# The end of a layer in a two-layer decoder trunk: norm rows by a broadcasting DMA, statistics by column halves, the last quarter later, and the next layer's first stages tile by tile

## The chip, the core and the metric

The program runs on one core of one Trainium2 chip, in one launch. The metric is device time in microseconds (us), the median of three runs. A profile of one execution was taken by the hardware profiler; a granted TensorE clock of 1.00 in it means the upper of that engine's two levels, 2.4 GHz, and 0.50 the lower one, 1.2 GHz.

## The reference, cut to what matters

```python
def mixer(x, w_in, ...):                      # three attentions of h = x @ w_in, gated and merged
    h = x @ w_in                              # x [256, 1024], w_in [1024, 5316]
    ...
    return merged @ w_o

def moe(x, ...):                              # 16 experts, best group of 4, top 2 in it
    ...
    for e in range(N_EXPERTS):
        he = jax.nn.silu(xt @ w_gate[e]) * (xt @ w_up[e])
        y = y + combine[:, e:e + 1] * (he @ w_down[e])
    return y

def layer_norm(x, g, b):
    mu = mean(x, -1);  var = mean((x - mu) ** 2, -1)
    return (x - mu) * rsqrt(var + 1e-5) * g + b

for l in range(2):
    x = layer_norm(ALPHA * x + mixer(x, ...), ln1_g[l], ln1_b[l])
    x = layer_norm(ALPHA * x + moe(x, ...), ln2_g[l], ln2_b[l])      # the change sits here
```

All is float32, 256 tokens by 1024 columns.

## The kernel before, in words

The 256 tokens are two tiles (t = 0, 1) of 128 partitions. `xt` holds x, 128 by 2 by 1024. A weight product with full precision is done in three passes: weights and x are each split into a rounded part and a rest (`hl` and `xh`, `xl`; the function `split` does a cast on ACT, then a subtraction on DVE, or on POOL with `sub=G`), and each tile gets high by high, low by high and high by low.

**Mixer.** A layer's mixer is 60 stages of a quarter weight chunk each; `stage(l, i)` splits the weights of stage i, LA stages ahead of its matmuls. Stages 0 and 1 are two k-pairs of the first chunk of `w_in`, 324 columns wide (the names `w_in_0` and `w_in_1` are the two halves of that chunk). `turn_x(j, t)` transposes four 128-column blocks of token tile t on PE and splits them into `xh` and `xl`; j = 0 serves stages 0 and 1, j = 1 stages 2 and 3. Before the first stage, `mixer` calls `turn_x(0, 0)`, `todo[0]`, `turn_x(0, 1)`, `todo[1]`, where `todo` is what the end of the layer before left over. `TURN` (L38) puts both `turn_x(1, t)` behind the first half of stage 1.

**MoE.** 16 experts go in 8 pairs p = 0..7; tokens are gathered by one-hot matmuls and scattered back by `add(p, t, h)`, which adds pair p's result to PSUM tile `o[t, h]` (token tile t, column half h of 512) by two matmuls of 512 columns. Names in the trace: `ps` is `o[0, h]`, `pm` is `o[1, h]` here, `yt` the expert results.

**Layer end.** `last()` adds pair 7, takes the statistics (`bn_stats`, one per tile and half; then `ln_scales`: two `bn_aggr` and an add on DVE, and a power on POOL that gives `rstd`). It also builds the norm's rows `gb` (gamma and beta repeated on all 128 partitions) by `ln_rows`, four PE transposes of a column of `gcol` each, and an ACT copy. Then every quarter (t, h) of x is normalised: `first` (PSUM minus the mean, times gamma) and `second` (times rstd, plus beta) on DVE. The quarter (1, 1) goes another way: ACT takes it from PSUM with scale rstd and bias `sh` (minus mean times rstd, by `ln_shift` on DVE), and two POOL `tensor_tensor` multiply by gamma and add beta. In layer 0 quarters (0, 1) and the handover go to the next mixer as `todo`; `warm(WARM[2], ..)` fills PE with 12 transposes of the identity while it waits. In layer 1 every finished quarter is stored by a DMA.

**What sets the order.** Each engine runs its instructions in the order in which the code issues them. All weight loads go on SP's queue, in the order of `pump`. At the end of the MoE stands a fallback for overflowing experts, `over()`, an If on a loaded number: SP, too, comes to it, and on its usual side SP waits until every load that it has issued has landed before it issues the next ones.

Every recorded operation has line L163 in the profile (L162 in the changed kernel), a load L221 (L220); so instructions are told apart by their names and forms.

Of the kernel before, what the change touches and what calls it, by code (L numbers as in the profile page):

```python
# [11 lines left out]
F32 = mybir.dt.float32  # L12
# [6 lines left out]
D = 1024  # L19
S = 256  # L20
T = 2
# [12 lines left out]
TOPK = 64  # L34
BACKLOG = 2.5
SLACK = -1.0
WARM = [38, 6, 12]
TURN = [1, 1]  # L38


QKV_CHUNKS = [(384, 708), (0, 384), (708, 1220), (1220, 1732), (1732, 2244)]
# [163 lines left out]
def kernel(ctx: ExitStack, tc: tile.TileContext, x, w_in, a_w_uk, a_w_uv, c_sinks, w_branch,  # L205
# [224 lines left out]
    def mixer(l, todo):  # L430
# [24 lines left out]

        for t in range(T):
            turn_x(0, t)
            later.setdefault((TURN[t] // 2, TURN[t] % 2), []).append(partial(turn_x, 1, t))
            for f in todo[t:t + 1]:
                f()  # L460

# [332 lines left out]
        for i, (c, q) in enumerate(stages):  # L794
            if c == 11 and q == 0:
                while busy():
                    assert any([t.step(True) for t in tracks])
                drop(2 + 2 + 1)
                target["o"] = 11
                pump()  # L800

                rwg = small(KD * NE, "rwg").rearrange("p (k e) -> p k e", k=KD)
                V.tensor_tensor(rwg, rw, gcol[:, 8 * l:8 * l + 8, None].to_broadcast([128, KD, NE]), op=OP.mult)
                rwb = work()
                r2 = rwb[:, 0:128].rearrange("p (k e) -> p k e", k=KD)
                V.tensor_tensor(r2, rw, gcol[:, 16 + 8 * l:24 + 8 * l, None].to_broadcast([128, KD, NE]), op=OP.mult)
                for z, r in enumerate((rwg, r2)):
                    V.tensor_reduce(rwb[:, 128 + NE * z:128 + NE * z + NE], r.rearrange("p k e -> p e k"), axis=AX.X, op=OP.add)
            if c == 12 and q == 0:
                p = psc()  # L810
                PE.matmul(p[:, 0:2 * NE], cc("one").to_broadcast([128, 128]), rwb[:, 128:128 + 2 * NE], start=True,
                          stop=True)
                rsum = small(2 * NE, "rsum")
                V.tensor_copy(rsum, p[:, 0:2 * NE])
# [19 lines left out]
                while c < 7 and f"e{c - 2}" not in done:  # L834
                    assert prep.step(True)
            if first:
                pa[c] = [pmm() for z in range(2 if c < len(chunks) - 1 else 4)]
            if i == len(stages) - 1:
                def piece(h, t):

# [97 lines left out]
    def moe(l, sc, lg, rsum):  # L938
# [325 lines left out]
        def last():  # L1264

            stats = [small(12, f"bm{t}") for t in range(T)]
            for h in range(2):
                for t in range(T):
                    add(7, t, h, stop=True)
                    V.bn_stats(stats[t][:, 6 * h:6 * h + 6], o[t, h])  # L1270

            gb = slot([128, 2, D], F32, "gb")

            def rows_(h):
                for j in range(2):
                    A.copy(gb[:, j, halves[h]], ln_rows(2 + j, l, h, ptp))

            for h in range(2):
                rows_(h)
            sc = ln_scales(stats)  # L1280
            z = {(t, h): xt[0][:, t, halves[h]] for t in range(T) for h in range(2)}
            ov = out[0].rearrange("(t p) d -> p t d", p=128)

            def first(t, h):
                V.scalar_tensor_tensor(z[t, h], o[t, h], sc[t][0], gb[:, 0, halves[h]], op0=OP.subtract, op1=OP.mult)

            def second(t, h):
                V.scalar_tensor_tensor(z[t, h], z[t, h], sc[t][1], gb[:, 1, halves[h]], op0=OP.mult, op1=OP.add)
                ready(t, h)

            def ready(t, h):
                if l == depth - 1:
                    load(ov[:, t, halves[h]], z[t, h])

            first(0, 0)
            if l + 1 < depth:
                warm(WARM[2], pmm)
            else:
                first(1, 0)
            sh = ln_shift(*sc[1])  # L1300
            A.activation(z[1, 1], o[1, 1], AF.Identity, bias=sh, scale=sc[1][1])
            second(0, 0)
            if l + 1 < depth:
                first(1, 0)
            second(1, 0)
            for j, op in enumerate((OP.mult, OP.add)):
                G.tensor_tensor(z[1, 1], z[1, 1], gb[:, j, halves[1]], op=op)
            drop(3)
            return partial(first, 0, 1), partial(second, 0, 1), partial(ready, 1, 1)

        for p in range(NE // 2):
            if p == 6:

                tc.mark_branch_hint_location(f"over{l}", engines=[mybir.EngineType.PE])
            if p == 1:
                target["o"] = 6
            if p == 2:
                target["o"] = 7
            if p == 3:
                target["o"] = 8  # L1320
            if p == 7:
                target["o"] = 16
                if l == depth - 1:
                    over()
                    drop(3)
                    clk.on = True
            pg, pu = pmm(), pmm()
            up_("g", p, pg)
            if p == 1:
                slot_maps(0)  # L1330
                turn(0)
            he = hts[p] = work(name="he")
            hv, gv, uv_ = he.rearrange("p (k q) -> p q k", k=4), *(z.rearrange("p (q k) -> p q k", k=4) for z in (pg, pu))
            A.activation(hv, gv, AF.Tanh, scale=0.5)
            V.scalar_tensor_tensor(hv, hv, 1.0, gv, op0=OP.add, op1=OP.mult)
            if p == 1:
                accumulator(0)
            if p == 7:
                scatter(2, 0)
            up_("u", p, pu)  # L1340
            V.tensor_tensor(hv, hv, uv_, op=OP.mult)
            if p == 1:
                onehot(1)
            if p == 7:
                scatter(2, 1)
            if p % 4 == 3:
                drop(2)
            if p == 3:
                gather(1)
            if p == 7:  # L1350
                if l < depth - 1:
                    over()
                    drop(3)
                    clk.on = True
            if p > 0:
                def between():
                    turn(p)
                    if p == 1:
                        accumulator(1)
                    if p == 2:  # L1360
                        slot_maps(1)
                        totals()
                    if p == 4:
                        stm.append(masked())
                    if 3 <= p < 7:
                        scatter((p - 3) // 2, (p - 3) % 2)
                    if p == 7:
                        parts.extend(apart())

                down(p - 1, between)  # L1370
        down(NE // 2 - 1, rest)
        for h in range(2):
            for t in range(T):
                add(6, t, h)
        if l + 1 < depth:
            for i in range(2):
                stage(l + 1, i, sub=G)
        return last()

    todo = ()  # L1380
# [29 lines left out]
```

## Time and profile before

| | us |
|---|---|
| median of 3 runs | 843.89 (843.61, 843.89, 846.78) |
| the profiled execution | 846.54, span 844.7 (1.84 us around the span) |
| TensorE busy | 815.4 (97%), mean granted clock 0.993 |
| VectorE, ScalarE, GpSimd busy | 432.5, 289.8, 98.0 |
| layer 0: mixer, then MoE | to about 200, then to about 420 |
| the boundary of the layers | about 417 to 432 |
| layer 1: mixer, then MoE, end | to about 619, about 834, 844.7 |

Times in the rows are microseconds from the start of the span. In a timeline row stand start, duration, engine, line, operation, result and operands with their names and shapes; "x2" puts instructions that follow each other in one row, and a bracket gives the idle time of the engine before it and what ended it. Engines: PE (TensorE), DVE (VectorE), ACT (ScalarE), POOL (GpSimd), SP (which issues the DMAs).

### The profile page before, as it was taken

Reading aid. Unit: us, or ns where it says so; the run is one execution under the profiler, and the core shown is the slowest. Engines: PE = TensorE matmul, PEld = TensorE weight load, DVE = VectorE, ACT = ScalarE, POOL = GpSimd, SP = SyncE. Lnnn points to the kernel's source line nnn. Section 1 sums busy time; section 2 is a strip of 40 time slices with the busy share of each in tenths; the row PEclk is TensorE's granted clock in tenths of the full one; section 3 lists DMA queues with packets and bytes.
Section 4 is the critical chain, followed back from the end, with each engine's and each line's share of the span. In section 5 each row is a group of like instructions: output and inputs, shape, how many; then the busy total and the mean of one; then the engine's idle time right before and its main releaser. Section 6 shows DMA issues by size and latency. Waiting matters only on the chain.

```text
span 844.7 us, 11443 instructions
## 1 busy us (share of the span) xinstructions
PE 815.4 (97%) x4413; PEld 507.3 (60%) x4413; DVE 432.5 (51%) x898; ACT 289.8 (34%) x507; POOL 98.0 (12%) x90
## 2 busy tenths in 40 slices
PE   7999999999999999997999999999999999999986
PEld 7888778889543443333488877788884434333333
DVE  5798565785332232223388976548761412322244
ACT  5445667344111221110355466654331112111112
POOL 0222221002030000000131232110030300000001
PEclk9999999999999999999999999999999999999998
DMA  9993336995599999999898424478948999999992
GB/s 314 336 385 132 123 127 205 393 350 199 216 421 419 419 419 419 419 419 419 323 386 298 163 77 151 150 258 345 357 177 313 419 420 419 419 419 420 418 411 84
DMA packets 65115, 265.24 MB, mean 314 GB/s; under 512 B 6880, under 2 KB 11168, under 8 KB 40992
## 3 DMA queue, kind: packets, MB, share of 16 engines
q1 hardware_dynamic: 64912, 264.39, 80.3%
q8 instruction: 36, 0.59, 0.3%
q14 instruction: 23, 0.19, 0.1%
q10 hardware_dynamic: 144, 0.07, 0.0%
HBM read 263.39 MB, written 1.05 MB: 313 GB/s over the span
## 4 chain that ended last, share of the span: by engine, by line
PE 42%; DMA 7%; DVE 3%; ACT 0%; POOL 0%; issue 0%; POOLq 0%; ACTq 0%; SPq 0%
PE pm L163 36%; DMA w_d<-in_moe_w_down_dram 5%; PE pt L163 3%; PE ps L163 3%; DMA w_u<-in_moe_w_up_dram 2%; DVE bm L163 1%; DVE acc L163 1%; DVE hl L163 0%; POOLq L1406 0%; POOL acc L163 0%; DVE sel L163 0%; ACT hl L163 0%; DVE mv L163 0%; DVE x1l L163 0%; ACT acc L163 0%
## 5 line engine op out<-in xcount | busy, mean ns | idle before, releaser
L163 PE MATMUL pm<-hl,xh 128*128 128x512 f32 (+2 forms) x704 | 227.2, 390 | 1.5 <-ACT hl L163 1.3
L163 PEld LDWEIGHTS pm<-hl,xh 128*128 128x128 f32 x704 | 131.9, 190 | 29.1 <-issue 4.2
L163 DVE TENSOR_TENSOR hl<-w_in,hl 128x1024 fp32r<-128x1024 f32 (+2 forms) x86 | 104.7, 1228 | 60.6 <-ACT hl L163 57.9
L163 PE MATMUL pm<-hl,xl 128*128 128x512 f32 (+2 forms) x352 | 134.0, 381 | 0.3 <-DVE xl L163 0.3
L163 PE MATMUL pm<-w_d,he 128*64 128x512 f32 x512 | 121.0, 604 | 4.2 <-DVEq L1196 2.8
L163 PE MATMUL pm<-w_g,xe 128*64 128x512 f32 x512 | 115.3, 594 | 3.4 <-DVEq L1196 1.7
L163 PE MATMUL pm<-w_u,xe 128*64 128x512 f32 x512 | 114.9, 593 | 1.5 <-DMA w_u<-in_moe_w_up_dram 1.5
L163 ACT CAST hl<-w_in 128x1024 fp32r<-128x1024 f32 (+2 forms) x88 | 85.7, 1001 | 5.7 <-DMA w_in<-in_w_in_dram 4.9
L163 PEld LDWEIGHTS pm<-w_g,xe 128*64 128x64 f32 x512 | 36.9, 137 | 76.6 <-issue 71.8
L163 PEld LDWEIGHTS pm<-w_u,xe 128*64 128x64 f32 x512 | 38.7, 137 | 73.3 <-issue 67.6
L163 PEld LDWEIGHTS pm<-w_d,he 128*64 128x64 f32 x512 | 37.3, 138 | 74.0 <-issue 67.8
L163 PEld LDWEIGHTS pm<-hl,xl 128*128 128x128 f32 x352 | 67.1, 191 | 10.1 <-DVE xl L163 0.5
L163 DVE SCALAR_TENSOR_TENSOR he<-he,pm 128x512 f32<-128x512 f32 x16 | 17.0, 1063 | 87.8 <-ACT he L163 78.9
L163 DVE TENSOR_TENSOR he<-he,pm 128x512 f32<-128x512 f32 x16 | 17.1, 1069 | 67.1 <-PE pm L163 67.1
L163 PE MATMUL pm<-hl,mh 128*128 128x256 f32 (+1 forms) x192 | 46.5, 325 | 0.0
L163 ACT COPY he<-pm 128x512 f32<-128x512 f32 x14 | 8.2, 587 | 109.7 <-PE pm L163 109.7
L163 ACT ACTIVATE he<-pm 128x512 f32<-128x512 f32 x16 | 17.3, 1080 | 80.8 <-PE pm L163 80.8
L163 DVE SCALAR_TENSOR_TENSOR yt<-pm,cs,yt 128x512 fp32r<-128x512 f32 x32 | 22.9, 747 | 43.0 <-ACT yt L163 42.1
L163 ACT ACTIVATE yt<-pm,cs 128x512 fp32r<-128x512 f32 x32 | 20.8, 686 | 67.4 <-PE pm L163 63.2
L163 POOL TENSOR_TENSOR un<-un,su 128x512 f32<-128x512 f32 x24 | 30.7, 1284 | 95.2 <-DVE su L163 56.9
L163 PE MATMUL pm<-hl,oh 128*128 128x512 f32 x128 | 41.3, 394 | 0.0
L163 POOL TENSOR_TENSOR rstd<-rs,cst 128x1 f32<-128x1 f32 (+1 forms) x6 | 4.2, 692 | 309.5 <-DVE rs L163 309.5
(198 smaller groups left out, 1039.6 us busy)
## 6 DMA issues: line engine op xcount, KB each, us to landing
w_g<-in_moe_w_gate_dram SPq DMA_DIRECT2D x64, 1024.0 KB, 13.6
w_u<-in_moe_w_up_dram SPq DMA_DIRECT2D x64, 1024.0 KB, 14.3
w_d<-in_moe_w_down_dram SPq DMA_DIRECT2D x60, 1024.0 KB, 19.0
w_in<-in_w_in_dram SPq DMA_DIRECT2D x36, 1024.0 KB, 13.4
w_br<-in_w_branch_dram SPq DMA_DIRECT2D x8, 1024.0 KB, 5.1
w_wo<-in_w_o_dram SPq DMA_DIRECT2D x8, 1024.0 KB, 5.0
w_d<-in_moe_w_down_dram SPq DMA_DIRECT2D x8, 512.0 KB, 17.1
w_in<-in_w_in_dram SPq DMA_DIRECT2D x4, 768.0 KB, 8.0
```

Source lines behind the costliest of these rows:

```text
L163: r = f(*args, **kw)
```

## The change

1. **Rows.** `gb` is loaded at pair 7 by two DMAs of 512 KB each, whose source has stride 0 over the partitions; `ln_rows` and the ACT copies go from the layer end.
2. **Statistics by column halves.** Pairs 6 and 7 are added for half 0, with its `bn_stats`, then for half 1.
3. **`sh` on POOL** (one `tensor_scalar`) in place of DVE.
4. **The last quarter.** Its ACT and POOL work, `other()`, comes in layer 0 behind the next layer's `turn_x(0, 0)` and `first(0, 1)`; in layer 1 it is issued right behind `sh`, ahead of `first(1, 0)`.
5. **`WARM[2]`** goes from 12 to 28.
6. **First stages tile by tile.** In both layers stages 0 and 1 are issued together: tile 0 of stage 0, tile 0 of stage 1, `turn_x(1, 0)`, tile 1 of stage 0, `turn_x(1, 1)`, tile 1 of stage 1 (six matmuls each). The attention fill that these stages called is left out there.

```diff
-WARM = [38, 6, 12]
-TURN = [1, 1]
+WARM = [38, 6, 28]
...
             turn_x(0, t)
-            later.setdefault((TURN[t] // 2, TURN[t] % 2), []).append(partial(turn_x, 1, t))
             for f in todo[t:t + 1]:
                 f()
...
+            if i < 2:
+                if i == 0:
+                    pa[c] = [pmm(), pmm()]
+                else:
+                    both = [(z, *staged.pop((l, z))) for z in range(2)]
+                    for t in range(T):
+                        for z, hl, n in both:
+                            for kk in range(2):
+                                k, ts = 2 * z + kk, slice(128 * t, 128 * t + 128)
+                                PE.matmul(pa[c][t][:, :n], xh[:, k, ts], hl[:, 0, kk, :n], start=(k == 0), stop=False)
+                                PE.matmul(pa[c][t][:, :n], xl[:, k, ts], hl[:, 0, kk, :n], start=False, stop=False)
+                                PE.matmul(pa[c][t][:, :n], xh[:, k, ts], hl[:, 1, kk, :n], start=False, stop=False)
+                            if t == 1 or z == 1:
+                                if t == 1:
+                                    drop()
+                                if not (t == 1 and z == 1):
+                                    turn_x(1, t)
+                stage(l, i + LA)
+                continue
...
             for h in range(2):
-                for t in range(T):
-                    add(7, t, h, stop=True)
-                    V.bn_stats(stats[t][:, 6 * h:6 * h + 6], o[t, h])
-
-            gb = slot([128, 2, D], F32, "gb")
-
-            def rows_(h):
-                for j in range(2):
-                    A.copy(gb[:, j, halves[h]], ln_rows(2 + j, l, h, ptp))
-
-            for h in range(2):
-                rows_(h)
+                for p in (6, 7):
+                    for t in range(T):
+                        add(p, t, h, stop=(p == 7))
+                        if p == 7:
+                            V.bn_stats(stats[t][:, 6 * h:6 * h + 6], o[t, h])
+            if l + 1 < depth:
+                for i in range(2):
+                    stage(l + 1, i, sub=G)
...
+            def other():
+                A.activation(z[1, 1], o[1, 1], AF.Identity, bias=sh, scale=sc[1][1])
+                for j, op in enumerate((OP.mult, OP.add)):
+                    G.tensor_tensor(z[1, 1], z[1, 1], gb[:, j, halves[1]], op=op)
+
             first(0, 0)
             if l + 1 < depth:
                 warm(WARM[2], pmm)
+            sh = small(1, "sh")
+            G.tensor_scalar(sh, sc[1][0], -1.0, sc[1][1], op0=OP.mult, op1=OP.mult)
+            if l + 1 == depth:
+                other()
+                first(1, 0)
+                second(0, 0)
             else:
-                first(1, 0)
-            sh = ln_shift(*sc[1])
-            A.activation(z[1, 1], o[1, 1], AF.Identity, bias=sh, scale=sc[1][1])
-            second(0, 0)
-            if l + 1 < depth:
+                second(0, 0)
                 first(1, 0)
             second(1, 0)
-            for j, op in enumerate((OP.mult, OP.add)):
-                G.tensor_tensor(z[1, 1], z[1, 1], gb[:, j, halves[1]], op=op)
             drop(3)
-            return partial(first, 0, 1), partial(second, 0, 1), partial(ready, 1, 1)
+            if l + 1 == depth:
+                return partial(first, 0, 1), partial(second, 0, 1), partial(ready, 1, 1)
+            def beside():
+                first(0, 1)
+                other()
+            return beside, partial(second, 0, 1)
...
             if p == 7:
                 scatter(2, 1)
+                gb = slot([128, 2, D], F32, "gb")
+                for j, r in enumerate((ln2_g, ln2_b)):
+                    load(gb[:, j], bass.AP(tensor=r.tensor, offset=r.offset + l * D, ap=[[0, 128], [1, D]]))
...
-        for h in range(2):
-            for t in range(T):
-                add(6, t, h)
-        if l + 1 < depth:
-            for i in range(2):
-                stage(l + 1, i, sub=G)
         return last()
```

On PE, at the end of layer 0's MoE, the last eight pairs of adding matmuls. Before (`yt_3309` is pair 6, `yt_3352` pair 7; `ps_3328`, `pm_3331` are half 0 and `ps_3334`, `pm_3337` half 1 of the two tiles):

```order
L163 MATMUL ps_3328<-yt_3309,stm_2689 128x512 x2
L163 MATMUL pm_3331<-yt_3309,stm_2689 128x512 x2
L163 MATMUL ps_3334<-yt_3309,stm_2689 128x512 x2
L163 MATMUL pm_3337<-yt_3309,stm_2689 128x512 x2
L163 MATMUL ps_3328<-yt_3352,stm_2689 128x512 x2
L163 MATMUL pm_3331<-yt_3352,stm_2689 128x512 x2
L163 MATMUL ps_3334<-yt_3352,stm_2689 128x512 x2
L163 MATMUL pm_3337<-yt_3352,stm_2689 128x512 x2
```

And now (`yt_3312` is pair 6, `yt_3355` pair 7):

```order
L162 MATMUL ps_3331<-yt_3312,stm_2689 128x512 x2
L162 MATMUL pm_3334<-yt_3312,stm_2689 128x512 x2
L162 MATMUL ps_3331<-yt_3355,stm_2689 128x512 x2
L162 MATMUL pm_3334<-yt_3355,stm_2689 128x512 x2
L162 MATMUL ps_3337<-yt_3312,stm_2689 128x512 x2
L162 MATMUL pm_3340<-yt_3312,stm_2689 128x512 x2
L162 MATMUL ps_3337<-yt_3355,stm_2689 128x512 x2
L162 MATMUL pm_3340<-yt_3355,stm_2689 128x512 x2
```

Half 0 of both tiles is complete after the fourth pair of matmuls, where it was after the sixth; the last pair is half 1 of tile 1 in both.

On SP, around the If at the end of layer 0's MoE (`w_d` are the last expert's weights, `w_in_0` the first half chunk of the next layer; `fi` is the number that the If asks). Before:

```order
L221 DMA w_d_1_1_2954<-in_moe_w_down_dram 128x2x512
L221 DMA w_d_1_0_2915<-in_moe_w_down_dram 128x2x512
L221 DMA w_d_1_1_2954<-in_moe_w_down_dram 128x2x512
L221 DMA w_in_0_2959<-in_w_in_dram 128x4x324
L1194 TENSOR_LOAD fi
```

And now:

```order
L220 DMA w_d_1_1_2954<-in_moe_w_down_dram 128x2x512
L220 DMA w_in_0_2959<-in_w_in_dram 128x4x324
L220 DMA gb<-in_ln_g_dram 128x1024
L220 DMA gb<-in_ln_b_dram 128x1024
L1212 TENSOR_LOAD fi
```

The two loads of the rows stand between the next layer's first half chunk and the If, so SP's wait at the If covers them as well. In layer 1 the If stands ahead of pair 7, and the two loads come behind it, ahead of the stores.

## Rows read from the trace of the kernel before

**Rows 1.** The page's first line.
```profile
span 844.7 us, 11443 instructions
```

**Rows 2.** The chain that ended last: start, length, engine, result, count.
```profile
419.66 2.49 DVE bm L163 x4
...
801.37 19.92 DMA w_d<-in_moe_w_down_dram
```

**Rows 3.** Timeline at the boundary of the layers, all engines.
```profile
417.06 0.73 PE L163 MATMUL ps<-yt,stm 128*128 128x512 f32 x2
...
418.65 3.12 POOL L163 TENSOR_TENSOR hl<-w_in,hl 128x648 fp32r<-128x648 f32 x2 [172.35 <-ACT hl L163]
...
420.37 0.61 PE L163 MATMUL pm<-yt,stm 128*128 128x512 f32 x2
...
422.68 0.71 POOL L163 TENSOR_TENSOR rstd<-rs,cst 128x2 f32<-128x2 f32 x1 [0.91 <-DVE rs L163]
...
423.07 1.47 PE L163 MATMUL pm<-cst 128*128 128x128 f32 x12
...
423.50 0.75 DVE L163 SCALAR_TENSOR_TENSOR acc<-acc,rstd,gb 128x512 f32<-128x512 f32 x1
423.75 0.79 ACT L163 ACTIVATE acc<-pm,sh,rstd 128x512 f32<-128x512 f32 x1
...
424.40 0.63 PE L163 MATMUL pt<-cst,acc 128*128 128x128 f32 x4
424.62 2.95 POOL L163 TENSOR_TENSOR acc<-acc,gb 128x512 f32<-128x512 f32 x2 [1.23 <-ACT acc L163]
424.95 1.48 DVE L163 SCALAR_TENSOR_TENSOR acc<-acc,rstd,gb 128x512 f32<-128x512 f32 x1
...
426.95 0.73 DVE L163 SCALAR_TENSOR_TENSOR acc<-ps,mv,gb 128x512 f32<-128x512 f32 x1
...
427.24 0.59 ACT L163 CAST xh<-pt 128x512 fp32r<-128x512 f32 x1 [1.59 <-PE pt L163]
427.73 0.73 ACT L163 CAST hl<-w_in 128x648 fp32r<-128x648 f32 x1
427.86 0.69 DVE L163 TENSOR_TENSOR xl<-pt,xh 128x512 fp32r<-128x512 f32 x1 [0.17 <-ACT xh L163]
...
430.70 0.39 PE L163 MATMUL pm<-hl,xh 128*128 128x324 f32 x1
...
431.96 0.31 PE L163 MATMUL pm<-hl,xh 128*128 128x324 f32 x1
```

**Rows 4.** GpSimd's one small scalar operation: count, least/mean/most ns, when.
```profile
L163 POOL TENSOR_SCALAR sink<-sinks x1: 262/262/262, 32.8 to 32.8; 128x16 f32<-128x16 f32 x1
```

**Rows 5.** Timeline of the two engines at the end of layer 1.
```profile
836.02 0.74 DVE L163 SCALAR_TENSOR_TENSOR acc<-ps,mv,gb 128x512 f32<-128x512 f32 x1
836.20 0.71 POOL L163 TENSOR_TENSOR rstd<-rs,cst 128x2 f32<-128x2 f32 x1 [174.51 <-DVE rs L163]
...
837.59 0.78 ACT L163 ACTIVATE acc<-pm,sh,rstd 128x512 f32<-128x512 f32 x1 [0.21 <-DVE sh L163]
...
838.44 3.16 POOL L163 TENSOR_TENSOR acc<-acc,gb 128x512 f32<-128x512 f32 x2 [1.54 <-ACT acc L163]
```

**Rows 6.** SP's first issue behind the If of layer 0.
```profile
413.64 0.93 SPq L221 DMA_DIRECT2D w_in<-in_w_in_dram  x2
```

**Rows 7.** Stretches: window, length, PE, PEld, DVE, ACT, POOL busy (count), clock, DMA share, GB/s.
```profile
21.00:22.00 1.00, 1.00 (x8) 1.00 (x7) 0.37 (x2) 0.00 (x0) 0.66 (x2) 1.00 0.76 139
...
412.00:414.00 2.00, 2.00 (x11) 1.17 (x11) 0.00 (x0) 0.00 (x0) 0.00 (x0) 1.00 0.09 30
...
424.00:426.00 2.00, 1.03 (x9) 0.72 (x7) 1.96 (x3) 1.12 (x2) 1.30 (x2) 1.00 1.05 390
...
610.00:630.00 20.00, 18.12 (x157) 17.63 (x156) 11.96 (x42) 8.41 (x14) 6.86 (x5) 1.00 0.44 164
...
825.00:826.00 1.00, 1.00 (x5) 0.82 (x6) 0.00 (x0) 0.00 (x0) 0.00 (x0) 1.00 0.56 209
```

More of the change, by code (lines that the diff above doesn't have):

```diff
@@ L836, in mixer @@
             if first:
-                pa[c] = [pmm() for z in range(2 if c < len(chunks) - 1 else 4)]
+                pa[c] = pa.get(c) or [pmm() for z in range(2 if c < len(chunks) - 1 else 4)]
             if i == len(stages) - 1:
```

## The prediction, made before the changed kernel ran

> **What bounds the kernel now.** I read the page first: the span is 844.7 us [rows 1] and TensorE is busy in 97% of it, so an edit pays only where PE stands still. Then the chain of waits: it is PE almost everywhere, but leaves PE at the two places that the change touches. At the boundary of the layers it runs through VectorE's four statistics, 2.49 us from 419.66 [rows 2]; the end of layer 1 has the same four. Late in layer 1 it runs along weight loads of some 20 us each [rows 2]. Last the timeline of the boundary: the adding matmuls end behind 420.37 and the first matmuls of the next layer run to 432.5 [rows 3]; between them DVE, ACT, POOL and PE wait for each other. So the change can gain a part of these 12 us and of the last 8 us of the program, and no more.
>
> **Part by part.** The sum is made against the profiled execution, 846.54 us (the span and 1.84 us around it), which lies 2.65 us above the median of 843.89; a difference is carried over to the median unchanged.
>
> *Statistics by halves.* Eight pairs of matmuls start at 417.06 to 420.37 [rows 3], one every 0.47 us. Four statistics that follow each other take 2.49 us, 0.62 each [rows 2], and before they can only begin behind the sixth pair, to end at 422.15. Now two of them lie beside pairs 5 to 7; the third starts when pair 7 is done, about 420.56, and the fourth ends at 421.84. That is 0.31 us, at each of the two layer ends, and everything behind the statistics starts so much earlier: rstd ends at 423.39 before [rows 3], now 423.08. It is no summand of its own but the start of the next two.
>
> *The rows by DMA.* The copies and transposes lie ahead of rstd's end, on ACT and PE, which wait there; taking them away gives nothing but free engines. What can be late next is the load itself. In layer 0 it stands on SP between the next layer's first half chunk and the If, where SP waits for all that it has issued. Before, SP issued again at 413.64 [rows 6], and in 412 to 414 the DMA engines moved 30 GB/s [rows 7]: they were idle. Two loads of 0.52 MB at the 390 GB/s of [rows 7] take 2.7 us, so the wait ends at 416.3 instead of 413.6. Two instructions can notice. The next half chunk's cast on ACT at 427.73 [rows 3] has some 8 us in hand. The second of the two weight splits that POOL does in 3.12 us from 418.65 [rows 3] follows a cast that comes behind this wait; POOL must be free for rstd at 422.37, so its second half (1.56) must start by 420.8, the cast ahead of it (0.73) by 420.1, SP's step (0.93, as its issue in [rows 6]) by 419.2. The transfer may take 5.6 us, then; beyond that each us costs one. In layer 1 the loads come when the last weights have landed, in 825 to 826 [rows 7], and the rows are wanted at 836.02 [rows 5]: 9 us. Cost 0; bounds 0 and what the second rival gives.
>
> *The boundary, step by step, from rstd at 423.08.* second(0,0) 423.11 to 423.87 (0.75, [rows 3]). The 28 transposes of the warm-up go at 0.111 us each (12 from 423.07 until 424.40, [rows 3]) and fill PE from 420.84 to 423.96; turn_x(0,0) follows at 424.05 instead of 424.40. second(1,0) takes 0.75 instead of the 1.48 from 424.95 [rows 3], which lay beside POOL's two operations of 2.95 from 424.62: POOL now has its work later. Then DVE has xl of tile 0 (0.69), first(0,1) (0.73), xl of tile 1 (0.69), which brings it to 427.4 [rows 3]. ACT does xh (0.59), then the last quarter (0.79, [rows 3]), so that POOL starts its multiplication at 426.1. Tile 0's twelve matmuls run from 425.9 at some 0.15 us each (the first matmul of this form starts at 430.70 and the ninth at 431.96, [rows 3]) to 427.7. Then PE waits for second(0,1), the quarter that turn_x(1,0) reads. Here stands a fork: DVE's second(0,1) is ready at 427.4, and POOL goes from its multiplication to its addition about then, too. Of two that meet, one is slowed: second(1,0) above took 1.48 beside POOL and 0.75 alone, while first, which reads PSUM, took 0.73 beside it (at 426.95, [rows 3]).
>  - DVE first: second(0,1) ends at 428.1, tile 1's first six matmuls, with turn_x(1,0) ahead of them, at 429.6, turn_x(1,1) and the last six at 431.0. Before, they ended at 432.5: minus 1.5 us.
>  - POOL first: second(0,1) ends at 429.4 and the last matmul at 432.3: minus 0.2 us.
>
> I take the first for the sum, since by the times above DVE comes to the point at or before POOL; the second is the first rival. The Trainium skill ("SBUF — State Buffer", section "SBUF: two separate sides") says that VectorE with two SBUF inputs and GpSimd share a pair of ports that whichever starts first holds for its whole instruction while the other is fully blocked. The trace agrees: 1.48 is 0.75 and a wait of the size of half of POOL's 2.95; by that rule it is the fork, and nothing between its two ends.
>
> *The end of layer 1.* rstd ends at 836.91 [rows 5], now 0.3 earlier. `sh` on POOL takes about 0.26 (the nearest POOL operation of one scalar kind, [rows 4]; on DVE it lay behind first(1,0)), and ACT's last quarter starts at 837.0 instead of 837.59 [rows 5]. POOL's two operations now meet DVE's second(0,0) and second(1,0), which they did not all do before; I let them end at 841.3 instead of 841.60 [rows 5]. Minus 0.3; bounds minus 0.6 (all of ACT's gain) and plus 0.1 (all of it given back at the shared port and a little more).
>
> *The rest.* The first stages of layer 0 are reordered too: PE waits there for weights, not for the order, 0 (plus or minus 0.3). The attention fill of layer 1 moves by a few slots; I see no row that prices it, 0, with 1 us to either side. The clock: in 424 to 426 PE is busy 1.03 of 2.00 us and the grant stays at 1.00 [rows 7]; the gaps by the times above (0.6 us ahead of turn_x(0,1), 0.4 behind tile 0's matmuls) are no longer than those there.
>
> Sum: 1.5 and 0.3, minus 1.8 us: 844.7 on the profiled execution's scale, **842.1** on the median's.
>
> **The rivals.**
>
> *POOL has the port first.* For it: POOL's addition follows its multiplication on the same engine with nothing to wait for, and my 427.4 rests on six durations in a row. Against it: that sum favours DVE by a hair. It gives minus 0.2 and minus 0.3: 843.4.
>
> *The broadcast is slow, and the kernel slower.* Place: SP's wait at the If of layer 0, then the same loads ahead of layer 1's end. No row shows a read of one 4 KB row 128 times. Price: 1 us for each us beyond 5.6; the gain of 1.8 is gone at 7.4 us. The slowest stretch of loads that I find with the engines mostly busy, 139 GB/s at 21 us [rows 7], would make it 7.5 us, and 844.0, no change. At half that, 15 us, layer 0 loses 9.4, and in layer 1 the rows land at 841.5 where they are wanted at 835.7: 857. Against it: the 128 pieces are 4 KB each and go over all the engines as a weight tile does. The Trainium skill ("DMA: Bandwidth & Descriptors", section "Latency and other measured facts") tells of copies that fell to half or less, 214 to 103 GB/s, when each partition's stream started a large power of two behind the one before, and supposes that all of them fall on the same channels of the memory. No run here shows a stride of 0; halving the 390 above would make 5.4 us, just inside the break-even.
>
> *The gain at the boundary is hidden.* From 741 to 821 us the chain is weight loads [rows 2]; if that stream ran on its own clock, 1.5 us earlier at 432 would only be waited off in layer 1's MoE. For it: those rows. Against it: in 610 to 630 the loads moved 164 GB/s at a share of 0.44 [rows 7], so the buffers were full and the stream starts when PE frees them, as early as PE is. It gives minus 0.3: 843.6.
>
> **How the numbers follow.** Forecast 842.1: 0.45, its own range 841.0 to 843.0 (1 us for the reordered attention, 0.3 each for layer 0's start and the end). POOL first, 843.4: 0.25. Hidden, 843.6: 0.12. Slow broadcast: 0.13, about half of it above 848.1. The last 0.05 are for effects of the order that no row shows, to either side. The range of 8 in 10 is 840.8 to 846.2: below, the forecast with all its bounds; above, the two small rivals with 1 us and the cheap part of the slow broadcast. A change of 0.5% (4.2 us) is about what a measurement can tell from none: faster than 839.7 has 0.03, slower than 848.1 has 0.08, between them 0.89.
>
> **What would show it.** The third statistic starting ahead of the last pair of matmuls' end, and rstd 0.3 us earlier behind them. The loads of `gb` landing within 5.6 us of their issue, and POOL's two weight splits still touching each other. second(1,0) at 0.75. second(0,1) at 0.75 (forecast) or 1.3 us and more (POOL first). The last of the first two stages' matmuls 1.5 us earlier behind the adding matmuls than before; and the start of layer 1's MoE earlier by as much, or not (hidden). The prediction is wrong if PE's time between the two ends of layer 1's mixer changes by over 1 us, or if the clock falls to 0.50 behind the boundary.

## The result, and the profile after

| | before | changed |
|---|---|---|
| median of 7 runs, us | 843.89 (843.14 to 846.82) | 851.40 (850.48 to 855.88) |
| the profiled execution, us | 846.54, span 844.7 | 855.88, span 854.1 |
| mean granted clock of the profiled execution | 0.993 | 0.988 |

The changed kernel is slower: ratio 1.0089, 95% interval 1.0071 to 1.0106. The sign was forecast wrong. The mean granted clock of an execution matters in what follows, since both kernels have executions with more or fewer stretches at the lower level (1.2 GHz): the other runs of the changed kernel have 0.991 or 0.992, its profiled one 0.988, and most runs of the kernel before 0.995 to 0.997. Executions are compared at like clocks below where that changes the reading.

I laid the two traces side by side by PE's instructions. Behind the same matmul the changed kernel is late by 0.5 us in layer 0's MoE, by 1.6 from the middle of layer 1's mixer on, by 4.9 in layer 1's MoE and by 9.5 at the end. The 0.5 hides a loss of 1.6 at layer 0's router, since this execution was 1.1 us ahead from its first stages on; the starts of all the traces here differ by such amounts, from 1.3 us ahead of the kernel before to 0.1 behind. So the places that cost are four, the two routers, the attention of layer 1 and its end, and the boundary of the layers is not one of them.

**The boundary** did nearly what the working said up to the fork. The timeline of the changed kernel there (columns as in [rows 3]):

```profile
420.84 0.62 PE L162 MATMUL pm<-yt,stm 128*128 128x512 f32 x2
421.05 0.70 DVE L162 BATCH_NORM_STATS2 bm<-ps 128x6 f32<-128x512 f32 x1 [0.52 <-PE ps L162]
...
421.30 3.22 PE L162 MATMUL pm<-cst 128*128 128x128 f32 x28
...
422.87 0.71 POOL L162 TENSOR_TENSOR rstd<-rs,cst 128x2 f32<-128x2 f32 x1 [0.62 <-DVE rs L162]
...
425.06 0.75 DVE L162 SCALAR_TENSOR_TENSOR acc<-acc,rstd,gb 128x512 f32<-128x512 f32 x1
...
426.46 2.65 POOL L162 TENSOR_TENSOR acc<-acc,gb 128x512 f32<-128x512 f32 x2 [1.96 <-ACT acc L162]
...
427.85 1.80 DVE L162 SCALAR_TENSOR_TENSOR acc<-acc,rstd,gb 128x512 f32<-128x512 f32 x1
...
429.80 0.63 PE L162 MATMUL pt<-cst,acc 128*128 128x128 f32 x4 [1.42 <-DVE acc L162]
...
432.34 0.46 PE L162 MATMUL pm<-hl,xh 128*128 128x324 f32 x2
```

The last of the two stages' matmuls is the first of the two in that row. The same in the kernel before:

```profile
432.40 0.45 PE L163 MATMUL pm<-hl,xh 128*128 128x324 f32 x2
```

The last pair of adding matmuls starts at 420.84 (420.37 in [rows 3]), and rstd ends 2.74 us behind that start instead of 3.02. second(1,0), at 425.06, takes 0.75. But second(0,1), at 427.85, takes 1.80, beside POOL's addition, the second of the two in the row at 426.46. That addition starts at 427.84, only 0.01 us ahead of it, and PE waits 1.42 us. The last of the two stages' matmuls starts 11.50 us behind the last pair's start, and before it was 12.03: half a microsecond gained, of which 0.3 is left sixteen matmuls further on.

**The end of layer 1.** Here some 4.6 us go. First the kernel before, then the changed one, around the matmuls of `rest`, which add the split copy of x (`ah`, `al`) to the PSUM tiles, and the yt of pair 6:

```profile
820.00 0.69 ACT L163 ACTIVATE yt<-pm,cs 128x512 fp32r<-128x512 f32 x1 [1.03 <-PE pm L163]
...
825.25 0.39 PE L163 MATMUL ps<-al,identr 128*128 128x512 f32 x1
825.48 0.40 PE L163 MATMUL pm<-ah,identr 128*128 128x512 f32 x1
...
830.54 0.74 PE L163 MATMUL ps<-yt,stm 128*128 128x512 f32 x2
```

```profile
830.25 0.39 PE L162 MATMUL ps<-al,identr 128*128 128x512 f32 x1
831.86 1.27 ACT L162 ACTIVATE yt<-pm,cs 128x512 fp32r<-128x512 f32 x2 [8.78 <-SPq L1214]
832.07 0.35 SPq L220 DMA_DIRECT2D gb<-in_ln_g_dram  x1
...
833.39 0.61 PE L162 MATMUL pm<-ah,identr 128*128 128x512 f32 x1 [2.75 <-DVE yt L162]
...
840.12 0.73 PE L162 MATMUL ps<-yt,stm 128*128 128x512 f32 x2
```

ACT stands still 8.78 us, and what ends it is SP: its wait at the If, until the last weights have landed. PE needs the PSUM buffer that this yt frees and stands still for 2.75 us. From the `ps<-al` matmul to the first adding matmul it is 9.87 us here and 5.29 before. The windows of the changed kernel (columns as in [rows 7]) show the clock behind that gap, and behind one at the router of layer 1:

```profile
620.00:640.00 20.00, 16.15 (x111) 13.05 (x110) 13.76 (x44) 8.35 (x13) 5.98 (x5) 0.91 0.31 106
...
833.00:837.00 4.00, 3.61 (x10) 1.94 (x12) 0.99 (x2) 0.13 (x1) 0.00 (x0) 0.58 0.70 262
```

**The router.** Behind the first norm of both layers PE waits for the router's mask `msk`, the end of a chain of small DVE operations (`pr`, `best`, `msk`), while POOL does subtractions of the split of x (`x1l`). Kernel before, then changed, layer 0 and 1:

```profile
208.04 0.23 DVE L163 TENSOR_TENSOR pr<-sel 128x64 f32<-128x64 f32 x1
...
210.63 0.41 PE L163 MATMUL pm<-msk,cst 128*128 128x32 f32 x2 [1.60 <-DVE msk L163]
...
627.37 0.41 PE L163 MATMUL pm<-msk,cst 128*128 128x32 f32 x2 [1.60 <-DVE msk L163]
```

```profile
205.22 3.24 POOL L162 TENSOR_TENSOR x1l<-xt,x1h 128x512 fp32r<-128x512 f32 x2 [0.88 <-ACT aff L162]
...
206.92 1.61 DVE L162 TENSOR_TENSOR pr<-sel 128x64 f32<-128x64 f32 x1
...
211.12 0.41 PE L162 MATMUL pm<-msk,cst 128*128 128x32 f32 x2 [3.21 <-DVE msk L162]
...
630.92 0.41 PE L162 MATMUL pm<-msk,cst 128*128 128x32 f32 x2 [3.57 <-DVE msk L162]
```

One small addition, `pr`, takes 1.61 us instead of 0.23 (1.60 in layer 1). POOL's second subtraction, of 1.54 us, started at 206.91, 0.01 us ahead of it; in the kernel before DVE was 0.01 us ahead in both layers. The diff doesn't touch this code.

**The attention of layer 1** is planned otherwise; one of its transposes now waits for POOL, where PE was busy without a gap before:

```profile
495.28 0.66 PE L162 MATMUL pt<-cst,un 128*128 128x128 f32 x4 [0.93 <-POOL un L162]
```

### The profile page after: what moved, and what is told of

It is laid out like the page before. It is cut to its first block, busy times and chain, and to the rows that moved or that the text cites. A ratio compares the mean times of both kernels' runs of the same rounds, so it can differ in the third digit from the quotient of the medians.

```text
span 854.1 us, 11405 instructions
## 1 busy us (share of the span) xinstructions
PE 815.8 (96%) x4397; PEld 506.1 (59%) x4397; DVE 432.5 (51%) x896; ACT 285.1 (33%) x499; POOL 98.1 (11%) x92
## 3 DMA queue, kind: packets, MB, share of 16 engines
HBM read 265.49 MB, written 1.05 MB: 312 GB/s over the span
## 5 line engine op out<-in xcount | busy, mean ns | idle before, releaser
L162 POOL TENSOR_TENSOR un<-un,su 128x512 f32<-128x512 f32 x24 | 32.6, 1365 | 94.5 <-DVE su L162 39.1
```

The costliest lines, as they stand in the source:

```text
L162: r = f(*args, **kw)
```

## The experiments

Each was timed in turns with the kernel before on the same chip. Medians are given against the changed kernel's 851.4, which was timed in another series, or against the kernel before in the same series; its median lay between 843.35 and 846.04 in these series, so a difference of a microsecond against 851.4 is not shown by the medians alone.

**1. The buffer of the norm rows taken late (layer 1).** Buffers come from one ring. Before, the order behind the If was `wov`, `ah`, `al`, yt of pair 6, yt of pair 7, `gb`; in the change `gb` comes second, and each of the others moves on by one. The loads stay at their place in SP's queue.

```diff
             if p == 7:
                 scatter(2, 1)
-                gb = slot([128, 2, D], F32, "gb")
-                for j, r in enumerate((ln2_g, ln2_b)):
-                    load(...)
+                if l < depth - 1:
+                    rows_in()          # the same three lines
...
         def last():
+            if l == depth - 1:
+                rows_in()
```

> The changed kernel, but in layer 1 the buffer for the norm rows is taken, and its two loads issued, at the start of the layer end instead of at pair 7; on SP's queue they stand at the same place, only the buffers behind them in the ring (those of the last two scatter results yt among them) go back by one. Theory A (the wait at the end): the changed kernel's ACT stands still until SP's wait at the If is over, because the yt of pair 6 takes a buffer whose last user is covered by that wait, and before it was the yt of pair 7. Then ACT's yt of pair 6 comes some 0.2 us after its matmuls, PE's 2.75 us gap ahead of the adding matmuls and the half clock behind it are gone, and the time falls by 4 to 5 us against the changed kernel, to about 847. Rival B (the loads themselves): the broadcast loads hold up SP or the DMA engines; they are still there, so the time stays at 851.

Measured: 845.88 (845.35 to 846.54, 12 runs), 5.5 less; ratio to before 1.0022 (1.0010 to 1.0034). The yt of pair 6 and the matmuls of `rest`, timeline of this run:

```profile
819.34 0.69 ACT L162 ACTIVATE yt<-pm,cs 128x512 fp32r<-128x512 f32 x1 [1.03 <-PE pm L162]
...
824.59 0.39 PE L162 MATMUL ps<-al,identr 128*128 128x512 f32 x1
824.82 0.40 PE L162 MATMUL pm<-ah,identr 128*128 128x512 f32 x1
```

ACT no longer waits for SP, and PE has no gap. Theory A holds and B falls, since both loads are still there: the buffer's place cost it, not the transfer.

**2. The old order of the first stages in layer 1.**

```diff
-            if i < 2:
+            if i < 2 and l == 0:
```

> The changed kernel with the old order of stages 0 and 1 (and the old place of the two turn_x) in layer 1 only; layer 0 keeps the new order. Theory A: the attention fill that the new order leaves out costs PE a gap of 0.93 us near 495 us and about 1.6 us until the end of layer 1's mixer, so this kernel gains some 1.5 us there; it loses what the new order gives at the boundary (0 to 0.5 us). About 850. Rival B: the order of the fill is worth nothing since PE is busy all the time, and the 1.6 us are the boundary's own: no change, 851.4, or up to 0.5 us more.

Measured: 849.79 (847.35 to 850.91, 6 runs), 1.6 less. PE's gap near 495 is gone. It fits A, though the medians alone would not carry it: the ratios to the kernel before are 1.0061 (1.0037 to 1.0084) here and 1.0089 (1.0071 to 1.0106) for the change.

**3. A gate at the router, ahead of POOL's second subtraction** (a POOL operation that reads `pr`).

```diff
-        low(G, 0, 4)
...
+        G.tensor_scalar(held_, pr[:, 0:1], 8.0, None, op0=OP.mult)
+        low(G, 0, 4)
         V.tensor_reduce(gsum[:, 4:12], ...)
```

> The changed kernel with one small POOL operation on the router's pr put ahead of POOL's second subtraction of the first norm, so that the subtraction can't start before DVE's addition pr is done; the result is the same. Theory A (a tie at the shared port): in the changed kernel POOL starts 9 ns ahead of DVE's pr and DVE is held 1.6 us, in the kernel before DVE was 9 ns ahead and took 0.23; PE then waits 3.2 to 3.6 us for the router instead of 1.6, in both layers, and in layer 1 the clock falls to one half behind it. With the tie taken away pr takes 0.23, each gap falls by about 1 to 1.6 us, and the time falls by 2 to 4 us, to 847.5 to 849.5. Rival B: the longer gap comes from something ahead of the router, and the gate only delays POOL: no gain, 851 to 852.

Measured: 855.84 (854.26 to 856.56), 4.4 more. A miss, and the timeline of DVE and POOL says why:

```profile
626.41 0.22 DVE L162 TENSOR_TENSOR pr<-sel 128x64 f32<-128x64 f32 x1
...
627.03 1.52 POOL L162 TENSOR_TENSOR x1l<-acc,x1h 128x512 fp32r<-128x512 f32 x1
...
627.45 1.15 DVE L162 SCALAR_TENSOR_TENSOR best<-gr,sel 128x32 f32<-128x32 f32 x1
...
629.06 1.51 POOL L162 TENSOR_TENSOR x1l<-acc,x1h 128x512 fp32r<-128x512 f32 x1 [0.51 <-ACT x1h L162]
...
629.27 1.34 DVE L162 TENSOR_SCALAR msk<-msk 128x32 f32<-128x32 f32 x1
```

`pr` takes 0.22, but now `best` (1.15) and `msk` (1.34) are held by the two subtractions that the gate had put beside them. The gap stayed, 3.6 us in layer 1 and 3.2 in layer 0. The mechanism was right and the place of the gate wrong.

**4. One more DVE operation ahead of `pr`, so that POOL starts first, in the kernel before.**

```diff
         pr = small(64, "pr")
+        V.tensor_scalar(pr[:, 0:1], sel[:, 0:1], 8.0, None, op0=OP.mult)
```

> The kernel before with one small DVE operation (some 0.07 us) ahead of the router's addition pr, so that POOL's second subtraction starts first. Theory A (tie at the shared port): pr takes 1.6 us instead of 0.23, PE's gap at the router grows from 1.6 to about 3.2 us in both layers, and the time rises by 2 to 4 us, to 846 to 848. Rival B: DVE has the time to spare and nothing follows; 844.

Measured: 850.03 (848.90 to 851.44, 6 runs) against 843.35, more than I expected. Layer 1, DVE and PE:

```profile
623.95 1.43 DVE L163 TENSOR_TENSOR pr<-sel 128x64 f32<-128x64 f32 x1
...
627.97 0.41 PE L163 MATMUL pm<-msk,cst 128*128 128x32 f32 x2 [3.22 <-DVE msk L163]
```

The two gaps are longer by 1.6 us each, 3.2 us; the rest of the 6.7 comes with a clock of 0.990 to 0.993, where the kernel before has 0.997 mostly. The code does not settle who wins: runs 1 and 2 have the changed kernel's code up to the first router, word for word, and run 12 up to the second; `pr` took 0.22 or 0.23 at both routers of all three. Of the nine traces whose router code is that of before, only the changed kernel's lost the tie.

**5. Both losses undone** (edits 1 and 2 together).

> The changed kernel with both losses that the first four runs point to undone: in layer 1 the norm rows' buffer is taken at the layer end, and layer 1 keeps the old order of stages 0 and 1. Theory A (two independent losses, 5.5 and 1.6 us by those runs): 851.4 less 7.1, 844.3, within 0.7 us of the kernel before. Rival B (the order's 1.6 us are only where the clock happened to fall, not the order): as with the late buffer alone, 845.9.

Measured: 844.66 (842.54 to 848.16, 12 runs), ratio 1.0001 (0.9986 to 1.0016): the loss is accounted for, within some 1.3 us either way by that interval. At a clock of 0.997 it took 842.54 to 843.11 (four runs) where the kernel before took 843.00 to 843.65: what is left of the change gains some 0.5 us.

**6. The gate behind the mask, in the kernel before.**

```diff
-        low(G, 0, 4)
...
         V.tensor_scalar(msk, msk, GONE, None, op0=OP.is_equal)
+        hold = small(1, "hold")
+        G.tensor_scalar(hold, msk[:, 0:1], 8.0, None, op0=OP.mult)
+        low(G, 0, 4)
```

> The kernel before with POOL's second and third subtraction of the first norm held until the router's mask msk is done (one small POOL operation that reads it); the result is the same. Theory A (the tie at the shared port): no DVE operation of the router meets a POOL one any more, pr takes 0.23 and best 0.19 (0.65 before), PE's gap ahead of the one-hot matmuls falls from 1.6 to about 1.1 us in both layers, and no execution falls into the slower group of 846 to 848: 842 to 842.8, with a narrower spread. Rival B (what POOL does later then stands in the way of DVE's own subtraction or of the gather): 844 or more.

Measured: 843.82 (841.99 to 846.95, 12 runs) against 843.86, ratio 0.9991 (0.9975 to 1.0007): by the medians inconclusive. PE's gap fell to 1.15 us in both layers as expected (layer 0 shown), and at 0.997 the runs took 841.99 to 842.34, some 1.1 us less than before; but half of them had a clock of 0.994 and less and took 845.3 and more, so the executions of 845 us and more did not go away with the tie.

```profile
209.59 0.41 PE L163 MATMUL pm<-msk,cst 128*128 128x32 f32 x2 [1.15 <-DVE msk L163]
```

**7. The last quarter behind second(0,1)**, on top of edit 1.

```diff
             def beside():
-                first(0, 1)
+                second(0, 1)
                 other()
-            return beside, partial(second, 0, 1)
+            return partial(first, 0, 1), beside
```

> As the run with the late buffer (845.9), but at the boundary of the layers the last quarter's ACT and POOL work is issued behind second(0, 1) instead of behind first(0, 1). Theory A (POOL had the shared port first): second(0, 1) takes 0.75 us instead of 1.80, PE's gap ahead of turn_x(1, 0) falls from 1.42 to about 0.3 us, some 0.5 us come back as a wait for the last quarter, and the time falls by 0.5 to 1 us: 845.0 to 845.4. Rival B (the gain is given back in full, since the last quarter is late now): 845.9.

Measured: 847.18 (846.35 to 848.99, 11 runs), 1.3 more than run 1. Timeline of DVE and PE:

```profile
424.73 0.74 DVE L162 SCALAR_TENSOR_TENSOR acc<-acc,rstd,gb 128x512 f32<-128x512 f32 x1
425.42 1.87 DVE L162 TENSOR_TENSOR hl<-w_in,hl 128x648 fp32r<-128x648 f32 x1
...
425.61 0.63 PE L162 MATMUL pt<-cst,acc 128*128 128x128 f32 x4 [0.36 <-DVE acc L162]
428.47 0.66 PE L162 MATMUL pt<-cst,acc 128*128 128x128 f32 x4 [1.33 <-POOL acc L162]
```

second(0,1) takes 0.74 and PE's gap falls to 0.36, but then PE waits 1.33 us for POOL's quarter: 1.69 us in all against 1.42. The price was not saved but moved, and DVE's next operation pays beside POOL (1.87). The last of the two stages' matmuls starts 11.98 us behind the last pair's start, 0.5 later than in run 1 (11.49). Rival B, and a little worse; the rest of the 1.3 is not shown to be the edit's, since this execution also had a stretch at half clock behind layer 1's router that run 1's had not.

**8. The loaded rows alone, on the kernel before** (both layers).

> The kernel before with the first part of the change alone: the norm rows by two broadcasting loads at pair 7, in both layers; everything else as before. Theory A: the wait at the end of layer 1 comes with it (the yt of pair 6 takes the buffer that waits for SP), PE stands still for some 2.7 us ahead of the adding matmuls and the clock falls behind that: 843.6 and 5 to 5.5, 848.5 to 849. Rival B: the wait needs the rest of the change too: 843 to 844.

Measured: 853.70 (853.28 to 855.82, 4 runs). The wait comes with this part alone. It costs more than I expected and than the whole change did, by PE's waits at both places (boundary, then end) and the clocks behind them:

```profile
421.18 0.63 PE L163 MATMUL pt<-cst,acc 128*128 128x128 f32 x4 [2.10 <-DVE acc L163]
423.27 1.09 PE L163 MATMUL pt<-cst,acc 128*128 128x128 f32 x4 [1.46 <-DVE acc L163]
...
830.20 0.79 PE L163 MATMUL pm<-ah,identr 128*128 128x512 f32 x1 [4.22 <-DVE yt L163]
```

```profile
420.00:440.00 20.00, 17.27 (x95) 16.39 (x96) 15.87 (x28) 8.44 (x13) 6.06 (x7) 0.83 1.05 385
820.00:840.00 20.00, 14.45 (x49) 6.23 (x48) 2.91 (x4) 2.65 (x4) 0.00 (x0) 0.83 0.47 164
```

Without the rows' sixteen transposes, and with 12 warm-up transposes instead of 28, PE stands idle before turn_x(0,0), and the clock, which is 1.00 there in both other kernels, falls. Why the wait at the end is 4.22 us here and 2.75 in the changed kernel is not shown.

**9. Losses undone, and the gate** (edits 1, 2 and 6; measured below, with run 10).

> The changed kernel with the two losses undone in layer 1 (late buffer, old order of the first stages) and with POOL's subtractions of the first norm held until the router's mask is done. Theory A: at the boundary it keeps the 0.5 us that statistics by halves, the later last quarter and the loaded rows gave, and takes 1.1 us from the router's two gaps: against executions of the kernel before at the same granted clock 1.6 us less (841.6 where the clock is 0.997), the median 841.6 to 844 by how many executions have a half-clock stretch. Rival B (no step of the change gains anything): as the kernel before with the gate alone, 842.1 at 0.997.

**10. The same with the rows by transposes** and 12 warm-up transposes; of the change the statistics by halves, `sh` on POOL, the later last quarter and layer 0's stage order stay.

> As the run with both losses undone and the gate, but the norm rows are made by PE transposes and ACT copies in both layers, as in the kernel before, with 12 warm-up transposes. Theory A: the loaded rows gain nothing by themselves, since the copies and transposes lay beside the statistics: the same time as with the loads, within 0.3 us, at the same granted clock (841.6 at 0.997). Rival B: ACT's copies hold up the last quarter or PE's transposes the first turn_x: 0.3 to 1 us more.

Measured: run 9 842.14 (841.46 to 846.55, 10 runs), ratio 0.9960 (0.9940 to 0.9979); run 10 842.01 (840.80 to 843.70, 12 runs), ratio 0.9958 (0.9939 to 0.9977). Both beat the kernel before, by less than half a per cent, and the changed one. The ratios flatter them, because 13 of the 27 runs of the kernel before had a clock of 0.995 and less and 846.4 us and more; at 0.997 and 0.998 it is 841.46 to 842.66 and 840.80 to 841.70 against 842.78 to 843.55, so 1 to 2 us. The rows by DMA gain nothing here and may cost some tenths.

**11. The tile-by-tile order alone, on the kernel before.**

> The kernel before with the last part of the change alone: stages 0 and 1 tile by tile in both layers. Theory A: layer 0 stays as it is, and in layer 1 the new order costs 1.2 to 1.6 us (0.5 at the boundary, where turn_x(1, 0) waits for second(0, 1), and the rest in the attention, whose fill comes by another plan): 843.8 and 1.4, 845.2. Rival B (the new order costs only beside the other parts): 843.8.

Measured: 845.34 (844.16 to 848.63, 12 runs); against 844.13 the ratio is 1.0005 (0.9987 to 1.0022), inconclusive by itself. At 0.997 and more it took 844.16 and 844.66, about 1.2 us over the kernel before, and the attention's gap is there, though at the boundary the last of the two stages' matmuls starts 11.52 us behind the last pair's start, 0.5 earlier than in the kernel before:

```profile
491.88 0.66 PE L163 MATMUL pt<-cst,un 128*128 128x128 f32 x4 [0.88 <-POOL un L163]
```

**12. PE kept busy in the wait at the end**, on the changed kernel.

```diff
+                    if l == depth - 1 and (t, h) == (0, 0):
+                        warm(24)
```

> The changed kernel with 24 transposes of the identity (0.11 us each, 2.7 us) put on PE in layer 1 at the place where it waits for the yt of pair 6; the wait itself stays. Theory A: of the 5.5 us that the late buffer won, 2.75 are PE's wait and some 1.7 the half clock that follows it; with PE busy in the wait the clock stays at 1.00 behind it and the time falls by 1.5 to 2 us, 851.4 to about 849.6. Rival B (the clock falls there for other reasons, or the half clock hides beside DVE): no change, 851.4, or more where the transposes run past the wait.

Measured: 848.66 (847.71 to 849.70, 12 runs), 2.7 less. The wait is as long as ever, but PE is busy in it, and the clock behind it stays:

```profile
825.19 0.39 PE L162 MATMUL ps<-al,identr 128*128 128x512 f32 x1
...
828.33 0.50 PE L162 MATMUL pm<-ah,identr 128*128 128x512 f32 x1
...
833.50 0.73 PE L162 MATMUL ps<-yt,stm 128*128 128x512 f32 x2
```

```profile
828.00:832.00 4.00, 3.88 (x18) 1.82 (x18) 0.93 (x2) 0.16 (x2) 0.00 (x0) 1.00 0.80 259
```

From `ps<-al` to the first adding matmul it is 8.31 us, against 9.87 in the changed kernel and 5.29 in run 1. So the late yt cost 4.6 us in the trace: 3.0 are the wait and 1.6 the clock. In the other three traces with the wait left empty (runs 2, 3 and 8) the clock fell behind it, too. The medians give 5.5 and 2.7; the difference may lie in the other mixes of clocks in those series, since their executions have no trace but one each.

## Why the prediction was wrong, by its own steps

- **Rows by DMA: the step that failed.** I asked when the rows land and who waits for SP, in layer 0 in detail, and for layer 1 only whether the loads come in time ("9 us. Cost 0"). They did. But taking the buffer earlier moved each later buffer on by one, and a wait for SP that lay harmlessly on pair 7's yt fell on pair 6's. Run 1: 5.5 us by the medians; 4.6 by the traces, 3.0 of it the wait and 1.6 the clock (run 12). That an allocation order is part of a change, I had not thought of at all, and no rival had it.
- **The slower rival** had SP's wait at the If as its place, but the wrong cause and layer: the broadcast is not slow. SP issued again at 416.63 against 413.64 in [rows 6], with everything 0.5 us later: 2.5 us for 1.05 MB, where I had put 2.7 from 390 GB/s. In layer 1 the loads landed 4.1 and 4.9 us after their issue at 832, and were wanted at 845.
- **The hidden gain**, the third rival, falls as well: where a run came earlier to layer 1's router than the kernel before, by 4.5 us in run 6, it was still 4.4 ahead when the span ended.
- **The tile-by-tile order.** Forecast minus 1.5 at the boundary and nothing in the attention; measured 0.3 to 0.5 gained at the boundary by all parts together, and 1.2 to 1.6 lost in layer 1 by the order (runs 2 and 11). At the boundary POOL had the port first, my first rival; its minus 0.2 came near. The working had the two engines meet at 427.4, and they did: POOL was ahead by 0.01 to 0.03 us in seven of the eight traces with this last quarter. Sums of times to 0.1 us could not tell that, so neither branch was more than a guess. What the other branch is worth is only hinted at. Run 7 moved the whole last quarter, which is another order, and lost; in run 10's trace, with the old order in layer 1, DVE was first (second(0,1) 0.74, POOL's addition 1.66), and the last of the stages' matmuls started at 11.22 behind the last pair, 0.3 earlier than in run 5 (11.50). The order itself gains nothing beside the other parts: it is 11.49 with it (run 1) and 11.50 without (run 5), though PE's gaps there are 0.5 us shorter without. The attention, which I had set to 0 with 1 us to either side, since no row priced it, has a gap of 0.9 us for POOL; the rest of the 1.2 to 1.6 no view here explains. I had also read the 1.48 of second(1,0) as 0.75 and a wait of half of POOL's 2.95; the wait is 0.73, a quarter of it.
- **Right:** the statistics (0.28 measured, 0.31 forecast), second(1,0) at 0.75, and the end of layer 1, where POOL's last quarter ends 7.36 us behind the start of the last adding matmuls and 7.71 before, minus 0.35 against the forecast 0.3. Of this only 0.1 reached the end of the span, which lies 10.7 us behind that start and 10.8 before.
- **Not in the sum:** the router. It is a tie that the code does not settle, lost twice in the profiled execution of the changed kernel. That can account, with the clock, for most of why it lies 4.5 us over the median: run 3, whose trace has both gaps as long, has the median 855.84. It is no effect of the change that I could show, and the changed kernel's other six runs have no trace. I had taken the kernel before as one level, where its runs differ by 3 us.

What stays open: why in a given execution the clock falls behind a gap and in the next it doesn't, with the same gap (2.75 to 2.77 us, starting between 393 and 398, in all fourteen traces, with 0.50 behind it in seven); and a third of a microsecond that the router's gap in layer 1 is longer in kernels with the loaded rows (1.93 in runs 1 and 5, 1.60 before).

## What to carry to other kernels

When a change takes a buffer from a shared ring at another place, list who gets which buffer afterwards and what its last user waits for: the wait can land on an instruction that the diff never names. A gap on PE can cost more than its length where the clock falls behind it (a wait of 3.0 us cost 4.6 here), so judge a removed filler by the gap that it leaves. And before you call a microsecond a gain, look whether two engines start within some nanoseconds of each other at a shared resource: such a tie can be worth more than the edit, as at the router here, and it was settled by an ordering that has one of them start when the other is through with its whole run (run 6).

## What the runs showed of the hardware that I had not expected

- A VectorE operation of 0.23 us took 1.60 and 1.61 beside a GpSimd one of 1.53 and 1.54 that had started 0.01 us earlier (changed kernel), and 1.43 beside one that had started 0.19 us earlier (run 4). Even `msk`, whose only tensor input is one small tile in SBUF, took 1.34 in run 3, and 0.18 in the kernel before. The Trainium skill ("SBUF — State Buffer", section "SBUF: two separate sides") has the rule, an exclusive lock for the whole instruction, for a VectorE operation with two SBUF inputs or in a 2-port mode. The rows of `pr`, which has two inputs, agree: it ended 0.08 us behind the GpSimd operation. They show that what is left of the other engine's instruction is the price, not the length of one's own.
- Two reads of one 4 KB row into all 128 partitions, 0.52 MB each, lengthened SP's wait in layer 0 by 2.5 us. With the weights landed, in layer 1, DMA moved 385 GB/s in the best microsecond of these reads (835 to 836), where [rows 7] has 390 for weights.
